# One decoder layer's dilated attention: the third group's blocks of 128 positions become pairs of 64, and the scheduler's transfer costs change

## The chip, the cores and the metric

One core of a Trainium2 chip runs the whole program. The metric is device time in microseconds of one execution, as a median of runs. Five engines work side by side and meet through semaphores: TensorE (PE, matrix products and transposes, with its weight loads as PEld), VectorE (DVE), ScalarE (ACT), GpSimd (POOL), and SyncE (SP), which only starts DMA transfers here.

## What is computed

A two-layer decoder trunk over 1024 positions of width 1024. Layer A is gated linear attention. Layer B, to which the change belongs, is dilated sliding-window attention of 8 query heads over 2 shared key and value heads, in three groups with windows 128, 512 and 2048 and dilations 1, 4 and 16. In each group the sequence is split into `dilation` interleaved sequences and each query sees the last `window // dilation` keys of its own; the groups' outputs are joined by a softmax over their log-sum-exps.

```python
def dilated_window_attention(q, k, v, window, dilation):
    ...
    scores = jnp.einsum('brnqgpe,brnkge->brngpqk', qb, kcat)
    ...
    band = (rel >= 0) & (rel <= w_sub)
    ...
    m = jnp.max(scores, axis=-1, keepdims=True)
    p = jnp.exp(scores - m)
    den = jnp.sum(p, axis=-1)
    o = jnp.einsum('brngpqk,brnkge->brnqgpe', p, vcat) / jnp.moveaxis(den, -1, 3)[..., None]
    lse = jnp.moveaxis(m[..., 0] + jnp.log(den), -1, 3)
    ...
```

```python
    wts = jax.nn.softmax(jnp.stack(lses, axis=0), axis=0)
    o = jnp.sum(wts[..., None] * jnp.stack(outs, axis=0), axis=0)
    o = o.reshape(bsz, s, SWA_OUT)
    return (o.astype(x.dtype) * jax.nn.silu(g)) @ w_out
```

With dilation 16 and 1024 positions, the third group has 16 sequences of 64 positions each, and its window covers a whole sequence: a query sees the keys of its own sequence up to itself, and no others.

## The kernel before

The program does not write its instruction order by hand. Every call (`S.tensor.matmul(...)`, `S.vector...`, `S.sync.dma_start(...)`) is recorded as an operation with the tiles it reads and writes, and `Sched.order` then plays the list through a model: each engine takes the ready operation that can start first, ties going to the earlier recorded one. `cost` gives each operation's duration in that model. A transfer's cost there is a size divided by a rate; the loop in `order` adds a landing time and a time for which SP is taken. The result is a fixed order on each engine; on the chip each engine then runs its list strictly in that order and waits wherever an input or a buffer is not there. Every emitted instruction carries the line of the one call that emits it, L441, so groups are told apart by tile names. `with S.group()` ties several calls into one operation, so that nothing comes between them.

A projection is a chain of float32r matmuls of 512 columns into a PSUM bank `acc`. Each product is split into three (`wh` times `x1h`, `wh` times `x1l`, `wl` times `x1h`), so a bank takes 24 of them. Attention products are float32 and are issued as two instructions each. Transposes go through TensorE in bfloat16 halves.

In layer B (`layer_b`) there are 8 units, one per query head. For unit u:

- `q_proj(u)` makes the queries Q of three groups; `rope` rotates them on VectorE and writes them, permuted to the group's order by `to_group`, on VectorE or GpSimd.
- `scores(u)` makes score blocks in PSUM (`lv`, two banks), adds the mask and takes the maximum on VectorE (the custom operation `P<-lv,rmask` for the third group), and exponentiates on ScalarE. Row maxima and sums go to DRAM and back (`sts`, `std`, `nat`), because groups order the positions differently, and come back as weights (`ew`, `cwd`, `cw`).
- `attend(u)` scales the blocks P by `cw`, turns them by transposes on TensorE (`ms<-identb,P`), copies the turned blocks out (`PT`), and multiplies with the values V into banks `po` (two). The third group's result is copied from `po` to `og` first; the first and second group then accumulate in the same two banks and are added to `og`.
- `g_proj(u)` and `close(u)` apply the gate.

The third group (`g == 2` in the code) puts two of the 16 sequences interleaved into one block of 128 positions: 8 blocks of 128 by 128, where the mask `rmask` hides every pair of positions of different sequences, half of the block. So a unit has 8 score products of 128 by 128, 16 transposes and 8 products with V of 128 by 128 for this group. Two score blocks' worth of banks and two rounds of turning are used (`step = 4`, `for hb in range(2)`).

At the end of the program `out_ln` makes the first half of the tokens with columns transposed, and `out_ln_rows` four blocks of 128 tokens (j = 4 to 7). A block has two banks of 24 matmuls each. Their results are added to the residual on VectorE (`rt<-res,acc`), measured (`BN_STATS`, `BN_AGGR`), normalised in two passes over two halves (`rt<-rt,lnmv,gam` and `rt<-rt,lnR,bet`) and sent out. For these blocks the output weight is split anew into `woh` and `wol`.

Of the kernel before, what the change touches and what calls it, by code (L numbers as in the profile page):

```python
# [139 lines left out]
class Sched:  # L140
# [108 lines left out]
    def order(self):  # L249
# [62 lines left out]
        while n_done < len(ops):  # L312
# [261 lines left out]
def trunk(tc, xT, wP, wA, wAv, wa, w2, b2, ng, wO, wK, wV, wB, wOB, lng, lnb,  # L574
# [534 lines left out]
    vd = [dram.tile([T, 256], F32, name=f"vd{i}") for i in range(2)]  # L1109
# [7 lines left out]
    def to_group(pg, g, half):  # L1117
        if g == 2:
            return pg.rearrange("p (b a n) -> p n a b", b=8, a=16)[:, half * 4:half * 4 + 4]
        n = 512 // DIL[g]  # L1120
        return pg.rearrange("p (r i) -> p i r", r=DIL[g])[:, half * n:half * n + n, :]

    def tok_view(ap, g):
        if g == 2:
            return ap.rearrange("p (n a b) -> p n a b", n=4, a=16)
        return ap.rearrange("p (i r) -> p i r", r=DIL[g])

    def layer_b(xs):
        bmask = hp.tile([128, 256], F32, name="bmask", bufs=1)
        S.sync.dma_start(bmask, bmask_d)  # L1130
        rmask = hp.tile([128, 128], F32, name="rmask", bufs=1)
# [29 lines left out]
        def proj_v(g):  # L1161
            stage = {}

            def evac(j, acc):
# [8 lines left out]
                if g == 2:  # L1173

                    S.sync.dma_start(vd[1].rearrange("(a n b) e -> n a b e", a=16, n=8)[j], dst)
                elif j % 4 == 3:
                    h = j // 4 * 512
                    S.sync.dma_start(vd[g - 1][h:h + 512, :].rearrange("(n p) e -> p n e", p=128),
                                      pg.rearrange("p (n e) -> p n e", n=4))
            project_tok(wV[g], xs, [(j, lambda x, j=j: blk(x, j)) for j in range(8)], evac)  # L1180

        def load_v(c, g):
            V[c][g] = page(p0, F32, f"V{c}{g}")
            src = vd[g - 1][:, c * 128:c * 128 + 128]
            if g == 1:
                for n in range(2):
                    S.sync.dma_start(
                        V[c][g].rearrange("p (r n e) -> p r n e", r=4, n=2)[:, :, n, :],
                        src[n * 512:n * 512 + 512, :].rearrange("(p r) e -> p r e", r=4))
# [29 lines left out]
        def reload_kv():  # L1219
            for g in range(3):  # L1220
# [10 lines left out]
              2: [(b * 128, b * 128, 128) for b in range(8)]}  # L1231
        U = [dict() for _ in range(8)]

# [20 lines left out]
        def scores(u):  # L1254
# [3 lines left out]
            for g in (2, 1, 0):  # L1258
                step = 4 if g == 2 else 2
                for j0 in range(0, 8, step):  # L1260
                    sc = ps.tile([128, 512], F32, name="lv", bufs=2)
                    p = small("P", "a", 13)
                    o = 0
                    for j in range(j0, j0 + step):
                        qc, kc, nk = BL[g][j]
                        col = column(g, j)
                        P[g, j] = p, o
# [16 lines left out]
            with S.landing(RUNS):  # L1284
# [3 lines left out]
                for s in range(2):  # L1288
                    S.sync.dma_start(dst[0, s].rearrange("(b a n) -> a b n", b=8, a=16), sts[:, s, 0:8])
                for s in range(2):  # L1290
                    S.sync.dma_start(nat[:, s, 1, :], dst[1, s].rearrange("(n a b) -> a n b", n=8, a=16))
            with S.landing(GATHER):
                for s in range(2):
                    S.sync.dma_start(nat[:, s, 0, :], dst[0, s].rearrange("(b p) -> p b", p=128))
# [17 lines left out]
            with S.landing(RUNS):  # L1312
                for g in range(2):
                    S.sync.dma_start(cwd[u][g].rearrange("(n a b) -> a n b", n=8, a=16), ew[:, g])
# [6 lines left out]
        def attend(u):  # L1321
# [153 lines left out]
def _arrays(inputs):  # L1475
# [54 lines left out]
    q, k = np.meshgrid(r(128), r(128), indexing="ij")  # L1530
    tq, tk = (128 * (i % 8) + 8 * (i // 8) for i in (q, k))
    a["rmask"] = np.where((tq % 16 == tk % 16) & (tk <= tq), f4(0), f4(NEG)).astype(f4)
# [28 lines left out]
```

## Time and profile before

| | |
|---|---|
| median of 3 runs | 1208.53 us (1208.48 to 1209.45) |
| the profiled execution | 1207.9 us |
| its span, first to last instruction | 1206.1 us |
| mean granted TensorE clock | 0.998 |
| PE busy | 1185.7 us, 98% of the span |
| PEld busy (beside PE) | 1017.2 us, 84% |
| DVE, ACT, POOL busy | 754.1, 529.9, 219.6 us |

The profiled execution's own time is 1.8 us over its span and 0.6 us under the median of the runs. Matmuls are pipelined: the printed duration of one (0.39 us for 512 columns) is its latency, and the time it takes from the engine is the distance from its start to the next start (0.23 us). A row of the timeline therefore tells its cost by the start of the row behind it.

### The profile page before, as it was taken

What the parts mean: (1) busy time and instruction counts of PE and PEld (TensorE: products, weight loads), DVE (VectorE), ACT (ScalarE), POOL (GpSimd) and SP (SyncE); (2) the same over time, 40 slices, a digit from 0 to 9 for tenths busy, and PEclk for the clock granted to TensorE, in tenths of its full rate; (3) what the DMA queues carried; (4) which work ended last, traced back from release to release, by engine and by line L of the source; (5) the groups of instructions that cost most, each with busy time, mean ns of one, the idle gap of its engine ahead of it and who ended that gap; (6) DMA issues with size and microseconds to landing.
All of it is one profiled execution on the core that took longest, in us unless ns stands there. A gap on an engine that the chain in (4) does not pass through costs nothing.

```text
span 1206.1 us, 20729 instructions
## 1 busy us (share of the span) xinstructions
PE 1185.7 (98%) x8340; PEld 1017.2 (84%) x8340; DVE 754.1 (63%) x1448; ACT 529.9 (44%) x1070; POOL 219.6 (18%) x145
## 2 busy tenths in 40 slices
PE   9999999999999999999999999999999999999996
PEld 7888978988988887789988888888888888888885
DVE  5482962943967698962255655564656566657468
ACT  5452534433563344422114554545362545456242
POOL 0011101211222122420031213040312130203200
PEclk9999999999999999999999999999999999999999
DMA  8102111111243462554411111111412020124545
GB/s 264 41 20 70 36 54 53 59 49 36 71 165 114 148 211 99 196 184 141 131 56 41 46 37 54 37 53 36 132 46 55 36 55 19 38 63 133 172 133 183
DMA packets 93648, 107.57 MB, mean 89 GB/s; under 512 B 43792, under 2 KB 63248, under 8 KB 93552
## 3 DMA queue, kind: packets, MB, share of 16 engines
q1 hardware_dynamic: 93552, 106.25, 28.3%
q8 instruction: 65, 1.06, 0.4%
q14 instruction: 31, 0.25, 0.1%
HBM read 85.06 MB, written 21.17 MB: 88 GB/s over the span
## 4 chain that ended last, share of the span: by engine, by line
PE 88%; DVE 8%; issue 2%; ACT 1%; DMA 1%; POOL 0%; SPq 0%; DVEq 0%; ACTq 0%; POOLq 0%
PE acc L441 62%; PE po L441 9%; PE lv L441 9%; PE ms L441 4%; PE pro L441 3%; DVE rt L441 2%; DVE X L441 2%; DVE wl L441 1%; DVE oT L441 1%; DVE x1l L441 1%; DMA xf<-in_xT 1%; ACT wh L441 0%; DMA cosT<-in_cos 0%; DVE t L441 0%; DVE sq L441 0%
## 5 line engine op out<-in xcount | busy, mean ns | idle before, releaser
L441 PE MATMUL acc<-x1h,wh 128*128 128x512 f32 x608 | 252.2, 415 | 2.0 <-DVE t L441 1.5
L441 PE MATMUL acc<-x1l,wh 128*128 128x512 f32 x608 | 237.5, 391 | 0.7 <-DVE x1l L441 0.6
L441 PE MATMUL acc<-x1h,wl 128*128 128x512 f32 x608 | 237.5, 391 | 0.0
L441 ACT ACTIVATE wh<-wf 128x1024 fp32r<-128x1024 f32 (+2 forms) x102 | 106.0, 1041 | 253.7 <-PE acc L441 201.6
L441 POOL TENSOR_TENSOR wl<-wf,wh 128x1024 fp32r<-128x1024 f32 x46 | 110.2, 2396 | 549.8 <-ACT wh L441 499.0
L441 PEld LDWEIGHTS acc<-x1h,wl 128*128 128x128 f32 x608 | 114.1, 188 | 24.4
L441 PEld LDWEIGHTS acc<-x1h,wh 128*128 128x128 f32 x608 | 114.5, 188 | 23.3 <-DVE t L441 2.0
L441 PEld LDWEIGHTS acc<-x1l,wh 128*128 128x128 f32 x608 | 114.5, 188 | 22.4 <-DVE x1l L441 1.7
L441 ACT ACTIVATE P<-P,sts 128x128 f32<-128x128 f32 (+1 forms) x192 | 84.9, 444 | 56.3 <-DVE sts L441 54.8
L441 DVE TENSOR_TENSOR wl<-wf,wh 128x1024 fp32r<-128x1024 f32 (+2 forms) x56 | 71.6, 1279 | 56.3 <-ACT wh L441 53.7
L441 DVE TENSOR_TENSOR t<-acc,cosT 128x512 f32<-128x512 f32 x60 | 41.3, 689 | 86.1 <-PE acc L441 79.7
L441 DVE TENSOR_TENSOR t<-acc,sinT 64x512 f32<-64x512 f32 x120 | 82.6, 688 | 2.0 <-ACT R L441 0.4
L441 PE MATMUL acc<-xh,wh 128*128 128x512 f32 x208 | 82.6, 397 | 0.0
L441 PE MATMUL acc<-xh,wl 128*128 128x512 f32 x208 | 81.1, 390 | 0.0
L441 PE MATMUL acc<-xl,wh 128*128 128x512 f32 x208 | 81.0, 389 | 0.0
L441 ACT ACTIVATE PT<-ms 128x512 uint16<-128x512 uint16 (+1 forms) x112 | 67.1, 679 | 30.1 <-PE ms L441 27.0
L441 PE MATMUL lv<-K,Q 128*128 128x256 f32 (+1 forms) x384 | 78.8, 324 | 0.0
L441 PE MATMUL acc<-wh,xh 128*128 128x256 f32 x256 | 75.6, 295 | 0.0
L441 PE MATMUL po<-PT,V 128*128 128x128 f32 (+1 forms) x464 | 73.3, 304 | 0.3 <-DVE PT L441 0.3
L441 DVE CUSTOM_DVE_ANT_0 P<-lv,bmask 128x256 f32<-128x256 f32 (+1 forms) x128 | 47.7, 382 | 40.3 <-PE lv L441 39.5
L441 PE MATMUL acc<-wl,xh 128*128 128x256 f32 x256 | 72.4, 283 | 0.3 <-issue 0.3
L441 PE MATMUL acc<-wh,xl 128*128 128x256 f32 x256 | 72.2, 282 | 0.0
(232 smaller groups left out, 2454.3 us busy)
## 6 DMA issues: line engine op xcount, KB each, us to landing
wf<-in_wB SPq DMA_DIRECT2D x32, 512.0 KB, 3.3
wf<-in_wO SPq DMA_DIRECT2D x16, 512.0 KB, 3.3
wf<-in_wOB SPq DMA_DIRECT2D x16, 512.0 KB, 3.8
wf<-in_wA SPq DMA_DIRECT2D x13, 512.0 KB, 3.2
wf<-in_wK SPq DMA_DIRECT2D x12, 512.0 KB, 3.4
wf<-in_wAv SPq DMA_DIRECT2D x8, 512.0 KB, 3.6
res<-in_xT SPq DMA_DIRECT2D x16, 256.0 KB, 2.7
wf<-in_wV SPq DMA_DIRECT2D x8, 512.0 KB, 3.8
```

Source lines behind the costliest of these rows:

```text
L441: getattr(handle[o.eng], meth)(*[conv(a) for a in args], **{k: conv(v) for k, v in kw.items()})
```

## The change

The third group's two sequences of a block are no longer interleaved. Its order of positions is now by sequence, so 16 pieces of 64 positions stand one behind another. Scores of a pair of sequences are two products of 64 by 64 that share the 128 rows of the contraction and write the lower and the upper 64 partitions of `lv`. All 16 stand in one group and one bank, in 8 blocks of 64 columns. Turning them takes 8 transposes, since a turned piece of 128 by 128 now holds four sequences. Products with V contract over 64 partitions: 16 products of 64 by 128 weights and 64 columns, alternating between the lower and the upper half of the partitions, each half writing its own `po` bank. Four copies of 256 columns take the place of two of 512. The mask is 64 columns wide.

The stores and loads that permute statistics and V follow the new order: V of the third group goes to two buffers of its own in DRAM, `nat` is loaded by 8 transfers rather than 4 per unit and `cwd` stored by 4 rather than 2. In the scheduler's model, transfers cost less time per byte, land sooner and take SP longer, and products that contract over 64 rows have a cost of their own.

```diff
@@ order
             if e == "SP":
                 dma_free = max(dma_free, st) + c
-                o.t1 = dma_free + 2.0
-                free[e] = st + 0.1
+                o.t1 = dma_free + 1.7
+                free[e] = st + 0.37
@@ cost
+        if args[1].shape[0] == 64:
+            return 0.12
         m = args[1].shape[1]
         return {32: 0.02, 64: 0.05}.get(m, 0.43)
     if e == "SP":
-        return 0.1 + int(_np.prod((outs + ins)[0].shape)) * 4 / 190e3
+        return 0.1 + int(_np.prod((outs + ins)[0].shape)) * 4 / 280e3
...
@@ to_group
         if g == 2:
-            return pg.rearrange("p (b a n) -> p n a b", b=8, a=16)[:, half * 4:half * 4 + 4]
+            return pg.rearrange("p (e a n) -> p n a e", e=16, a=8)[:, half * 4:half * 4 + 4]
...
@@ load_v
-                S.sync.dma_start(V[c][g].rearrange("p (b e) -> p b e", b=8),
-                                  src.rearrange("(p b) e -> p b e", b=8))
+                src = vd3[c].rearrange("(n a s k j) e -> k s a n (j e)", n=8, a=8, s=2, k=2)
+                for k in range(2):
+                    for s in range(2):
+                        S.sync.dma_start(V[c][g][k * 64:k * 64 + 64, s * 512:s * 512 + 512], src[k, s])
...
@@ scores
-                step = 4 if g == 2 else 2
+                step = 8 if g == 2 else 2
...
+                    if g == 2:
+                        with S.group():
+                            for j in range(8):
+                                for s in range(2):
+                                    x = s * 512 + j * 64
+                                    o = place(j)
+                                    S.tensor.matmul(sc[s * 64:s * 64 + 64, o:o + 64], Q[g][:, x:x + 64],
+                                                     Kc[g][:, x:x + 64], start=True, stop=True)
...
-                        S.tensor.matmul(sc[:, o:o + nk], Q[g][:, qc:qc + 128], Kc[g][:, kc:kc + nk],
-                                         start=True, stop=True)
+                        if g < 2:
+                            S.tensor.matmul(sc[:, o:o + nk], Q[g][:, qc:qc + 128], Kc[g][:, kc:kc + nk],
+                                             start=True, stop=True)
...
@@ attend
-            for hb in range(2):
-                t = turn([(4 * hb + s, 0) for s in range(4)], 2)
-                po = ps.tile([128, 512], F32, name="po", bufs=2)
-                for s in range(4):
-                    S.tensor.matmul(blk(po, s), blk(Vc[2], 4 * hb + s), t[:, s, :], start=True, stop=True)
-                S.vector.tensor_copy(og.rearrange("p (n a b) -> p a n b", n=8, a=16)[:, :, :, 4 * hb:4 * hb + 4],
-                                      po.rearrange("p (b a n) -> p a n b", b=4, a=16))
+            p, t = P[2, 0][0], small("PT", "d", 4)
+            turn_blocks(t, [p.halves(BF)[:, :, i * 128:i * 128 + 128] for i in range(4)])
+            po = [ps.tile([128, 512], F32, name="po", bufs=2) for _ in range(2)]
+            with S.group():
+                for s in range(2):
+                    for j in range(4):
+                        for k in range(2):
+                            h = slice(k * 64, k * 64 + 64)
+                            S.tensor.matmul(po[k][:, s * 256 + j * 64:s * 256 + j * 64 + 64],
+                                             blk(Vc[2], s * 4 + j)[h], t[h, j * 128 + s * 64:j * 128 + s * 64 + 64],
+                                             start=True, stop=True)
+            for k in range(2):
+                for s in range(2):
+                    x = s * 8 + k * 4
+                    S.vector.tensor_copy(
+                        og.rearrange("p (n a e) -> p n a e", n=8, a=8)[:, :, :, x:x + 4],
+                        po[k][:, s * 256:s * 256 + 256].rearrange("p (j a n) -> p n a j", j=4, a=8))
...
```

**Where instructions stand.** First TensorE, in `attend` of unit 0, with the scores of unit 1 among it (`ms<-identb,P` are transposes, `po<-PT,V` products with V, `lv<-K,Q` scores, `acc` projections). Before:

```order
L441 MATMUL acc<-x1h_4468,wl 128x512
L441 MATMUL po<-PT,V_6118 128x128 x4
...
L441 MATMUL po<-PT,V_6118 128x128 x4
...
L441 MATMUL po<-PT,V_5795 128x128 x3
L441 MATMUL lv<-K_5040,Q 128x128
...
L441 MATMUL po<-PT,V_5795 128x128 x9
```

Now, from the same projection on:

```order
L441 MATMUL acc<-x1h_4468,wl 128x512
...
L441 MATMUL po<-PT,V_6070 128x64 x16
...
L441 MATMUL lv<-K_5045,Q 64x64 x16
L441 MATMUL po<-PT,V_5732 128x128 x12
...
L441 MATMUL lv<-K_4967,Q 128x128 x2
```

The lines left out are transposes: 6 and 12 and 6 before; 6 ahead of and 12 behind the `128x64` products now. All of the third group's products with V now stand in one piece, and the next unit's third-group scores in another, ahead of the second group's first use of the `po` banks.

Then VectorE, at the same place in unit 0. Before:

```order
L441 TENSOR_TENSOR t_6672<-acc,cosT 128x512
L441 TENSOR_TENSOR t_6687<-acc,sinT 64x512 x2
L441 COPY og<-po 128x16x8x4 x2
L441 COPY PT<-ms 128x384 x2
L441 ISA P,sts<-lv,rmask 128x128
```

Now:

```order
L441 TENSOR_TENSOR t_6684<-acc,cosT 128x512
L441 TENSOR_TENSOR t_6697<-acc,sinT 64x512 x2
L441 COPY PT<-ms 128x384
L441 TENSOR_TENSOR Q<-t_6684,t_6697 128x4x8x16
L441 COPY og<-po 128x64x4 x4
L441 ISA P,sts<-lv,rmask 128x64
```

The permuted write of the third group's Q has come from GpSimd to VectorE, ahead of the copies that set the `po` banks free.

Last VectorE at the end of the program, the last rows of its list. Before:

```order
L441 SCALAR_TENSOR_TENSOR rt<-res,acc 128x512
L441 BN_STATS lnst<-rt 128x6
L441 BN_AGGR lnmv<-lnst 128x2
L441 SCALAR_TENSOR_TENSOR rt<-rt,lnmv,gam 128x512 x2
L441 SCALAR_TENSOR_TENSOR rt<-rt,lnR,bet 128x512 x2
L441 BN_AGGR lnmv<-lnst 128x2
L441 SCALAR_TENSOR_TENSOR rt<-rt,lnmv,gam 128x512 x2
L441 SCALAR_TENSOR_TENSOR rt<-rt,lnR,bet 128x512 x2
```

Now:

```order
L441 SCALAR_TENSOR_TENSOR rt<-res,po 128x512
L441 BN_STATS lnst<-rt 128x6
L441 SCALAR_TENSOR_TENSOR rt<-rt,lnmv,gam 128x512 x2
L441 SCALAR_TENSOR_TENSOR rt<-rt,lnR,bet 128x512 x2
L441 SCALAR_TENSOR_TENSOR rt<-res,acc 128x512
L441 BN_STATS lnst<-rt 128x6
L441 BN_AGGR lnmv<-lnst 128x2
L441 SCALAR_TENSOR_TENSOR rt<-rt,lnmv,gam 128x512 x2
L441 SCALAR_TENSOR_TENSOR rt<-rt,lnR,bet 128x512 x2
```

Behind the last matmuls' result (`rt<-res,acc`) two blocks were normalised; now it is one. The splits `wol<-wf,woh`, of which five stood behind `sum<-lnA,sum` on VectorE, have moved: three stand there now.

## Rows read from the trace of the kernel before

**Rows 1.** Page: busy time, share and count by engine; chain's shares by engine.
```profile
PE 1185.7 (98%) x8340; PEld 1017.2 (84%) x8340; DVE 754.1 (63%) x1448; ACT 529.9 (44%) x1070; POOL 219.6 (18%) x145
...
PE 88%; DVE 8%; issue 2%; ACT 1%; DMA 1%; POOL 0%; SPq 0%; DVEq 0%; ACTq 0%; POOLq 0%
```

**Rows 2.** Chain that ended last, in order of time: start us, us, what.
```profile
710.96 32.68 PE acc L441 x144
...
1075.43 18.39 PE acc L441 x81
...
1097.80 1.82 DVE P L441 x4
```

**Rows 3.** Timeline of PE, third group's scores: start us, us, instructions merged.
```profile
634.86 0.60 PE L441 MATMUL lv<-K,Q 128*128 128x128 f32 x4
...
636.00 0.60 PE L441 MATMUL lv<-K,Q 128*128 128x128 f32 x4
```

**Rows 4.** Timeline of PE, third group's turning and products with V.
```profile
679.67 1.07 PE L441 MATMUL ms<-identb,P 128*128 128x128 bf16 x16
680.54 0.48 PE L441 MATMUL acc<-x1h,wh 128*128 128x512 f32 x1
...
682.04 1.16 PE L441 MATMUL po<-PT,V 128*128 128x128 f32 x8
683.03 0.50 PE L441 MATMUL ms<-identb,P 128*128 128x128 bf16 x6
683.37 1.11 PE L441 MATMUL po<-PT,V 128*128 128x128 f32 x8
684.32 0.86 PE L441 MATMUL ms<-identb,P 128*128 128x128 bf16 x12
```

**Rows 5.** Timeline of PE, layer A: eight 64 by 64 products on two column halves.
```profile
308.44 0.28 PE L441 MATMUL acc<-wh,xl 128*128 128x256 f32 x1
308.64 0.69 PE L441 MATMUL lv<-X 128*64 128x64 f32 x16
...
309.48 0.28 PE L441 MATMUL acc<-wl,xh 128*128 128x256 f32 x1
```

**Rows 6.** Groups by form: engine, rows*columns, size, xcount | busy us, mean ns | idle.
```profile
L441 PE MATMUL lv<-X 128*64 128x64 f32 x64 | 2.7, 227 | 1.9 <-DVE X L441 1.9
...
L441 PEld LDWEIGHTS lv<-X 128*32 128x32 f32 x1408 | 15.5, 110 | 6.4 <-issue 2.7 <-ACT X L441 1.7
...
L441 PEld LDWEIGHTS po<-PT,V 128*128 128x128 f32 x464 | 64.6, 191 | 8.3 <-ACT PT L441 4.2 <-DVE PT L441 0.5
```

**Rows 7.** Groups by form: copies out of PSUM, and GpSimd's permuted write of Q.
```profile
L441 DVE COPY v<-acc 128x256 f32<-128x256 f32 x16 | 6.6, 413 | 0.2 <-PE acc L441 0.2
...
L441 DVE COPY og<-po 128x512 f32<-128x512 f32 x16 | 11.0, 690 | 14.5 <-PE po L441 14.5
...
L441 POOL TENSOR_TENSOR Q<-t,t 128x512 f32<-128x512 f32 x17 | 21.9, 1288 | 34.4 <-DVE t L441 34.4
```

**Rows 8.** Timeline of VectorE and TensorE at the program's end, last matmul last.
```profile
1195.88 0.68 DVE L441 SCALAR_TENSOR_TENSOR rt<-res,acc 128x512 f32<-128x512 f32 x1
...
1197.43 1.41 DVE L441 SCALAR_TENSOR_TENSOR rt<-rt,lnmv,gam 128x512 f32<-128x512 f32 x2
1198.76 1.41 DVE L441 SCALAR_TENSOR_TENSOR rt<-rt,lnR,bet 128x512 f32<-128x512 f32 x2
1200.09 0.20 DVE L441 BATCH_NORM_AGGREGATE lnmv<-lnst 128x2 f32<-128x12 f32 x1
...
1201.66 1.41 DVE L441 SCALAR_TENSOR_TENSOR rt<-rt,lnR,bet 128x512 f32<-128x512 f32 x2
...
1195.37 0.39 PE L441 MATMUL acc<-woh,ogl 128*128 128x512 f32 x1
```

**Rows 9.** A late stretch: its length, busy us of PE, PEld, DVE, ACT, POOL, clock.
```profile
1180.00:1196.00 16.00, 15.76 (x70) 12.72 (x68) 15.80 (x28) 4.64 (x9) 0.00 (x0) 1.00 0.56 196
```

**Rows 10.** Timeline of SP: one issue of a transfer.
```profile
1175.39 0.34 SPq L441 DMA_DIRECT2D res<-x1t  x1
```

More of the change, by code (lines that the diff above doesn't have):

```diff
@@ L1107, in trunk @@
     kvd = [dram.tile([128, T], F32, name=f"kvd{i}") for i in range(4)]
-    vd = [dram.tile([T, 256], F32, name=f"vd{i}") for i in range(2)]
+    vd = dram.tile([T, 256], F32, name="vd")
+    vd3 = [dram.tile([T, 128], F32, name=f"vd3{c}") for c in range(2)]
     ogB = [dram.tile([128, T], F32, name=f"ogB{k}") for k in range(NK)]
@@ L1124, in tok_view @@
         if g == 2:
-            return ap.rearrange("p (n a b) -> p n a b", n=4, a=16)
+            return ap.rearrange("p (n a e) -> p n a e", n=4, a=8)
         return ap.rearrange("p (i r) -> p i r", r=DIL[g])
@@ L1130, in layer_b @@
         S.sync.dma_start(bmask, bmask_d)
-        rmask = hp.tile([128, 128], F32, name="rmask", bufs=1)
+        rmask = hp.tile([128, 64], F32, name="rmask", bufs=1)
         S.sync.dma_start(rmask, rmask_d)
@@ L1172, in evac @@
                     S.vector.tensor_copy(dst, acc)
-                if g == 2:
-                    S.sync.dma_start(vd[1].rearrange("(a n b) e -> n a b e", a=16, n=8)[j], dst)
-                elif j % 4 == 3:
+                if j % 4 == 3:
                     h = j // 4 * 512
-                    S.sync.dma_start(vd[g - 1][h:h + 512, :].rearrange("(n p) e -> p n e", p=128),
-                                      pg.rearrange("p (n e) -> p n e", n=4))
+                    rows = pg.rearrange("p (n e) -> p n e", n=4)
+                    if g == 1:
+                        S.sync.dma_start(vd[h:h + 512, :].rearrange("(n p) e -> p n e", p=128), rows)
+                    else:
+                        for c in range(2):
+                            S.sync.dma_start(vd3[c][h:h + 512, :].rearrange("(n p) e -> p n e", p=128),
+                                              rows[:, :, c * 128:c * 128 + 128])
             project_tok(wV[g], xs, [(j, lambda x, j=j: blk(x, j)) for j in range(8)], evac)
@@ L1183, in load_v @@
             V[c][g] = page(p0, F32, f"V{c}{g}")
-            src = vd[g - 1][:, c * 128:c * 128 + 128]
             if g == 1:
@@ L1230, in layer_b, with place @@
               1: [(r * 256 + n * 128, r * 256, 128 + 128 * n) for r in range(4) for n in range(2)],
-              2: [(b * 128, b * 128, 128) for b in range(8)]}
+              2: [(b * 64, b * 64, 64) for b in range(8)]}
         U = [dict() for _ in range(8)]
+        def place(b):
+            return b % 4 * 128 + b // 4 * 64
         def column(g, j):
@@ L1288, in scores @@
                 for s in range(2):
-                    S.sync.dma_start(dst[0, s].rearrange("(b a n) -> a b n", b=8, a=16), sts[:, s, 0:8])
+                    S.sync.dma_start(dst[0, s].rearrange("(e a n) -> a e n", e=16, a=8), sts[:, s, 0:8])
                 for s in range(2):
-                    S.sync.dma_start(nat[:, s, 1, :], dst[1, s].rearrange("(n a b) -> a n b", n=8, a=16))
-            with S.landing(GATHER):
+                    for i in range(2):
+                        S.sync.dma_start(nat[i * 64:i * 64 + 64, s, 1, :],
+                                          dst[1, s].rearrange("(n a i b) -> i a n b", n=8, a=8, i=2)[i])
+            with S.landing(GATHER / 2):
                 for s in range(2):
-                    S.sync.dma_start(nat[:, s, 0, :], dst[0, s].rearrange("(b p) -> p b", p=128))
+                    for i in range(2):
+                        S.sync.dma_start(nat[i * 64:i * 64 + 64, s, 0, :],
+                                          dst[0, s].rearrange("(i b p) -> i p b", i=2, b=8)[i])
             mn = hp.tile([128, 8], F32, name="mnB", bufs=1)
@@ L1313, in scores @@
                 for g in range(2):
-                    S.sync.dma_start(cwd[u][g].rearrange("(n a b) -> a n b", n=8, a=16), ew[:, g])
+                    for i in range(2):
+                        S.sync.dma_start(cwd[u][g].rearrange("(n a i b) -> i a n b", n=8, a=8, i=2)[i],
+                                          ew[i * 64:i * 64 + 64, g])
             with S.landing(GATHER):
@@ L1529, in _arrays @@
     a["bmask"] = np.where((rel >= 0) & (rel <= 128), f4(0), f4(NEG)).astype(f4)
-    q, k = np.meshgrid(r(128), r(128), indexing="ij")
-    tq, tk = (128 * (i % 8) + 8 * (i // 8) for i in (q, k))
-    a["rmask"] = np.where((tq % 16 == tk % 16) & (tk <= tq), f4(0), f4(NEG)).astype(f4)
+    q, k = np.meshgrid(r(128) % 64, r(64), indexing="ij")
+    tq, tk = (128 * (i % 8) + 16 * (i // 8) for i in (q, k))
+    a["rmask"] = np.where(tk <= tq, f4(0), f4(NEG)).astype(f4)
     return a
```

4 lines of the change are left out of this document (3 added, 1 removed).

## The prediction

> **What bounds the kernel now.** I read the page's busy times first: TensorE is busy for 1185.7 of 1206.1 us, and the chain that ended last lies on it for 88% [rows 1]. A busy TensorE need not be one that is used without gaps, so next I read its timeline for the distances from start to start. In the chain, 144 projection matmuls follow each other in 32.68 us [rows 2], 0.227 us each, and that is what they cost wherever I looked in layer B. There is hardly a place there where the engine waits: in the units' stretches the next instruction's inputs are there before the one ahead is through. So in layer B a microsecond taken from TensorE is a microsecond of the program, if nothing that now hides behind it comes out. The exception is the end: the last matmul starts at 1195.37, VectorE takes up its result at 1195.88 and works until 1201.66 + 1.41 = 1203.07 [rows 8]. In the 16 us up to that point VectorE is busy for 15.80 [rows 9]. So VectorE sets the end there, and the order of its list counts.
>
> **Scores of the third group.** Before, two of the eight products with three projection matmuls behind them take 636.00 - 634.86 = 1.14 us [rows 3]; less 3 x 0.227 that is 0.46 for two, 1.84 for eight. The new products have a relative in layer A that is the same in form: 64 by 64 with 128 rows of contraction, alternating between two column halves. Eight of them (16 instructions) stand between matmuls of 256 columns. From the start of the last such matmul ahead of them to that of the second behind them is 309.48 - 308.44 = 1.04 us [rows 5]; without the group these two starts would be two steps of 0.12 us apart, 256 columns at half of the 0.227 for 512 and a little, so the group costs 0.80. Of it, (0.69 - 0.227) / 15 = 0.031 us is what one more instruction adds [rows 5, 6], and 0.80 - 16 x 0.031 = 0.31 is what it costs to go to halves and back. Two halves at once are seen here: an instruction of 128 columns takes 0.46 / 4 = 0.115 above, so one of 64 would take some 0.06 if alone. Sixteen products are 32 instructions: 0.80 + 16 x 0.031 = 1.30. Gain 0.54 a unit; with twice the whole group's price (1.60) it would be 0.24.
>
> **Transposes.** Sixteen take 680.54 - 679.67 = 0.87 us [rows 4], 0.054 each. Eight are left out: gain 0.43 a unit. Half the copies of turned blocks go too, on ScalarE, beside TensorE: nothing.
>
> **Products with V.** Before: 0.99 and 0.95 us for four each [rows 4], 1.94 for the eight, 0.121 per instruction. After: 32 instructions with half the columns, half the contraction and a full-width weight load (64 rows by 128 columns) each. No row of the trace shows products on two row halves. The bounds: as good as two column halves, 32 x 0.031 + 0.31 = 1.30; no better than now per instruction, 32 x 0.121 + 0.31 = 4.18. What lies between is told by the weight loads. They last 110 ns for 32 columns and 191 ns for 128 [rows 6], 0.84 ns for each column, so some 0.108 us for 128 columns if only the part that grows with the columns occupies the array. That is nearly the 0.121 that a full-size instruction takes now, so halving the columns that stream through cannot bring the distance down as long as one half is loaded at a time. If the two row halves load and compute beside each other, as the two column halves do, a pair takes what one instruction takes now: 16 x 0.121 + 0.31 = 2.25. I take this value, a loss of 0.31 a unit, because halves of the array are seen to run together in the one direction that is shown, while the load stays full width.
>
> The Trainium skill, "TensorE: Matmul & The Clock Gate", section "LDWEIGHTS (loading the stationary operand)", speaks against this part of the change: a load takes about its columns divided by 1.2 in ns, whether 32 or 128 rows are filled. The trace agrees on the columns (0.84 ns each), and says nothing on the rows. By this rule alone, with loads one behind another, the 32 loads would take an estimated 3.4 us, and the sum below would come out slower than before.
>
> A unit then gains 0.54 + 0.43 - 0.31 = 0.66 us, and eight units 5.3 us.
>
> **What must stay hidden.** (a) The two `po` banks. Both are now held until four copies of 256 columns have passed, and the second group's products come next. TensorE has 12 transposes (0.65) and the next unit's third-group scores (1.30) ahead of them, 1.95 us. The copies start about 0.2 after the products, as now, and take 4 x 0.413 [rows 7]: the first bank is free after 1.0 us, the second after 1.85, wanted after 2.2. Covered, by 0.3. (b) The write of Q, 1.29 us on GpSimd so far [rows 7], now stands on VectorE ahead of those copies; from the start of the turning to the end of the products it is 684.32 - 679.67 = 4.65 us in the trace [rows 4], and it is done within them if it takes VectorE no longer than GpSimd: covered too. (c) Six more transfers of statistics and weights a unit, 0.34 us each to issue [rows 10]: 2.1 us more, in a path that lies on the chain in the last unit alone, where four scalings of P by `cw` on VectorE follow a run of 81 projection matmuls [rows 2]. There the changed list has 99 of them as cover: 18 x 0.227 = 4.1 us more. Covered. (d) The refitted costs of transfers act through order alone. Up to layer B the lists are almost the same, with shifts of three matmuls where TensorE already waits for the layer norm; I set this at nothing, with 1 us either way.
>
> **The end.** Behind the last result VectorE normalises two blocks before and one now. What goes from behind it is one pair of passes, 1200.09 - 1197.43 = 2.66 us [rows 8]. That holds if VectorE is not late by then: it has two splits of weights fewer in the last 40 us, and the block ahead has its two passes (2.7 us) and one result to take up (two instructions of 0.7) in the 5.4 us of the last bank's 24 matmuls. I take the 2.66 whole; the bounds are 0 and 2.66.
>
> Sum: 5.3 + 2.7 = 8.0 us off 1207.9, so 1199.9 for an execution like the profiled one; the runs' median stands 0.6 above that one, so **1200.5 us**.
>
> **Rivals.**
> *The halves cost no more than column halves.* Products with V take 1.30: a unit gains 0.54 + 0.43 + 0.64 = 1.61, eight 12.9, with the end 15.6: 1192.9. For it: the same array, the same number of passes, and the loads of column halves do overlap. Against it: there the loads are half as wide.
> *The row halves take turns.* 32 x 0.121 + 0.31 = 4.18 for V, a loss of 2.24 a unit: 2.24 - 0.97 = 1.27 more a unit, 10.2 in all, less the end's 2.7: 1216.0, slower. The change would then not do what its name says. The point from which it decides: 32p + 0.31 must exceed 1.94 + 0.97 + 0.33 (an eighth of the end), which is p = 0.092 us per instruction. For it: the loads' width and the price above. Against it: the column halves do run together.
> *The copies uncover `po`.* If a copy of 256 columns with its strided write takes as long as one of 512 (0.69) [rows 7], the second bank is free after 0.2 + 4 x 0.69 = 2.96 us, 0.77 later than wanted; eight units lose 6.2, and the time is 1206.7, no change. A late write of Q on VectorE would act in the same way. Against it: 512 columns in the same kind of pattern take the same 0.69 as plain copies do.
> *The end is not shortened* (VectorE late): 1203.2, still faster; this lies in the forecast's range.
>
> **How the numbers follow.** The forecast with its scatter (1197 to 1204) has 0.55, the cheap halves 0.17, the turns 0.16, the uncovered banks 0.12. About 0.2% (2.4 us) is what a measurement of this kernel can tell from no change. Faster by more takes the forecast, the cheap halves and the better part of the third: 0.77. Within: most of the rest of the uncovered banks, 0.08. Slower: 0.15. The range leaves out the turns and a little of the others: 1191.5 to 1208.
>
> **What would show it.** In the changed profile: the third group's 32 score instructions 0.03 us apart; the 32 products with V 0.06 apart on average (0.03 or 0.12 in the rivals); eight transposes fewer a unit; no idle time of TensorE ahead of `po<-PT,V 128x128` with VectorE's `og` copies as its end; last VectorE instruction ending 4.5 us after the last result is taken up, not 7.2. The prediction is wrong in kind if TensorE begins to wait in the units for statistics or for Q.

## The result, and the profile after

| | before | after |
|---|---|---|
| median | 1208.99 us (1208.48 to 1209.57, 4 runs) | 1201.92 us (1200.40 to 1202.50, 4 runs) |
| ratio | | 0.9939, 95% interval 0.9922 to 0.9957 |
| the profiled execution | 1207.9 | 1202.5 |
| its span | 1206.1 | 1200.6 |
| mean granted TensorE clock | 0.998 | 0.995 |

The kernel became 7.1 us faster by the medians. The two profiled executions differ by 5.5 us in span; they are one run each, and the one of after is among its slower ones. The start of the program alone varies by up to 1.8 us between executions of one list: the 500th matmul of 512 columns starts at 195.98 us here and at 194.18 in `e8_quarters_priced`, whose lists are the same up to there.

The page of after, busy time by engine, which answers [rows 1]:

```profile
PE 1179.5 (98%) x8532; PEld 1008.6 (84%) x8532; DVE 777.4 (65%) x1480; ACT 515.1 (43%) x1061; POOL 188.7 (16%) x122
```

**A unit.** The timeline of TensorE in unit 0's `attend`, with the scores of the next unit behind it (columns as in [rows 3, 4]: start us, us, merged instructions):

```profile
684.53 0.49 PE L441 MATMUL ms<-identb,P 128*128 128x128 bf16 x6
684.95 2.00 PE L441 MATMUL po<-PT,V 64*128 64x64 f32 x32
686.89 0.84 PE L441 MATMUL ms<-identb,P 128*128 128x128 bf16 x12
687.66 1.15 PE L441 MATMUL lv<-K,Q 128*64 128x64 f32 x32
688.74 2.94 PE L441 MATMUL po<-PT,V 128*128 128x128 f32 x24
```

From start to start the 32 products with V take 686.89 - 684.95 = 1.94 us, 0.061 each. The trace starts them in pairs: two instructions 7 ns apart, then 105 ns to the next two, 0.111 us a pair. The 32 score instructions take 1.08 us, 0.034 each. No row shows TensorE waiting.

How long a whole unit takes is read from the chain that ended last, where the long run of projections comes back once a unit (start us, us, what). After:

```profile
709.08 36.08 PE acc L441 x159
...
771.92 36.07 PE acc L441 x159
...
834.76 36.08 PE acc L441 x159
```

That is 62.84 us twice. Before, the run of 144 that starts at 710.96 [rows 2] comes back at 774.78, after 63.82 us. A unit gives 0.98 us. Summing all start-to-start distances of one such unit by kind shows where:

| in one unit, us | before | after | gain |
|---|---|---|---|
| products with V, third group | 2.06 (16 instructions) | 1.93 (32) | 0.12 |
| scores, third group | 1.50 (16) | 1.08 (32) | 0.42 |
| transposes | 3.92 (70) | 3.65 (62) | 0.27 |
| projections (the same 192) | 45.55 | 45.26 | 0.29 |
| everything else of groups 1 and 2 | 10.80 | 10.91 | -0.11 |

(The V row of before is the difference of 46 and 30 instructions of one form, the score row that of 26 and 10.) The projections are the same matmuls; they lose fewer switches, since the third group stands in one piece instead of being spread among them.

**Where time was lost.** The 3428 matmuls of 512 columns are the same in both kernels, so the start of the n-th can be compared. At the 1250th (470 us) after is 0.35 us ahead. At the 1310th (486 us) it is 4.52 behind, by the first scores 3.04 behind. Eight units bring it to 4.96 ahead (1099 us), and the last matmul starts 3.24 ahead. In between lie two places where TensorE waits. The first is layer B's layer norm. TensorE's waits from 440 to 520 us (what waits, for whom: us in total, times, longest), before:

```profile
PE acc L441 <- DVE t L441: 1.5, 2, 1.1
PE ms L441 <- POOL sum L441: 1.1, 1, 1.1
```

and after:

```profile
PE ms L441 <- DVE sum L441: 2.0, 1, 2.0
PE acc L441 <- DVE t L441: 1.7, 2, 1.0
PE ms L441 <- ACT sum L441: 1.4, 1, 1.4
```

VectorE's list there has changed: two splits of weights (`wl<-wf,wh`) come ahead of `rt<-rt,mean`, and the last sum runs on VectorE while GpSimd splits weights. Windows of the same place (length, busy us of PE, PEld, DVE, ACT, POOL, granted clock, DMA), before:

```profile
477.00:483.00 6.00, 6.00 (x29) 4.93 (x28) 5.88 (x9) 2.45 (x4) 0.90 (x1) 1.00 0.27 91
```

and after:

```profile
470.00:477.00 7.00, 3.60 (x15) 2.48 (x13) 5.73 (x7) 2.21 (x3) 2.35 (x1) 0.93 0.23 75
477.00:483.00 6.00, 5.37 (x13) 3.86 (x14) 5.65 (x10) 1.94 (x3) 0.00 (x0) 0.51 0.28 87
```

TensorE was idle for half of 470 to 477, and behind that, from 477 to 483, its clock was granted at 0.51, the 1.2 GHz level; ten matmuls stand 0.427 us apart there instead of 0.227. The second place is the last unit, where the four copies out of `po` stand behind seven scalings of P. After, TensorE's and VectorE's timelines:

```profile
1095.71 0.49 PE L441 MATMUL ms<-identb,P 128*128 128x128 bf16 x6 [0.38 <-ACT PT L441]
1096.93 0.49 PE L441 MATMUL po<-PT,V 128*128 128x128 f32 x2 [0.72 <-DVE og L441]
1097.59 0.71 PE L441 MATMUL po<-PT,V 128*128 128x128 f32 x4 [0.17 <-DVE og L441]
```

```profile
1091.47 4.75 DVE L441 TENSOR_SCALAR P<-P,cw 128x128 f32<-128x128 f32 x7
1096.13 1.41 DVE L441 COPY og<-po 128x256 f32<-128x256 f32 x4
```

**The end**, which answers [rows 8]:

```profile
1192.13 0.39 PE L441 MATMUL acc<-woh,ogl 128*128 128x512 f32 x1
```

```profile
1192.56 0.69 DVE L441 SCALAR_TENSOR_TENSOR rt<-res,acc 128x512 f32<-128x512 f32 x1 [0.77 <-PE acc L441]
1193.28 0.69 DVE L441 BATCH_NORM_STATS2 lnst<-rt 128x6 f32<-128x512 f32 x1
1194.01 0.21 DVE L441 BATCH_NORM_AGGREGATE lnmv<-lnst 128x2 f32<-128x12 f32 x1
1194.25 1.42 DVE L441 SCALAR_TENSOR_TENSOR rt<-rt,lnmv,gam 128x512 f32<-128x512 f32 x2
1195.58 1.41 DVE L441 SCALAR_TENSOR_TENSOR rt<-rt,lnR,bet 128x512 f32<-128x512 f32 x2
```

VectorE ends 1196.99 - 1192.56 = 4.43 us after it takes up the last result, 7.19 before [rows 8]. It now waits 0.77 us for that result, so it is no longer late.

The ledger of the two profiled executions, in us gained: 0.35 up to the layer norm, -3.4 at the layer norm and until the first scores, +8.0 in the units, -1.7 from there to the last matmul, +2.8 in VectorE's end, -0.6 behind it. Sum 5.5.

### The profile page after: what moved, and what is told of

The parts are those of the page before. It is cut to its first block, busy times and chain, and to the rows that moved or that the text cites. A ratio compares the mean times of both kernels' runs of the same rounds, so it can differ in the third digit from the quotient of the medians.

```text
span 1200.6 us, 21156 instructions
## 1 busy us (share of the span) xinstructions
PE 1179.5 (98%) x8532; PEld 1008.6 (84%) x8532; DVE 777.4 (65%) x1480; ACT 515.1 (43%) x1061; POOL 188.7 (16%) x122
## 4 chain that ended last, share of the span: by engine, by line
PE 53%; DVE 2%; DMA 1%; issue 1%; ACT 0%; DVEq 0%
PE acc L441 38%; PE po L441 7%; PE lv L441 6%; PE ms L441 3%; DMA wf<-in_wOB 1%; DVE P L441 0%; DVE rt L441 0%; DVE wol L441 0%; ACT woh L441 0%; DVE t L441 0%; DVE wl L441 0%; DVE PT L441 0%; DVE og L441 0%; DVE lnA L441 0%; DVE lnst L441 0%
## 5 line engine op out<-in xcount | busy, mean ns | idle before, releaser
L441 POOL TENSOR_TENSOR wl<-wf,wh 128x1024 fp32r<-128x1024 f32 x45 | 107.7, 2395 | 608.0 <-ACT wh L441 573.6
L441 DVE TENSOR_TENSOR wl<-wf,wh 128x1024 fp32r<-128x1024 f32 (+2 forms) x57 | 74.2, 1302 | 67.0 <-ACT wh L441 66.5
L441 ACT ACTIVATE P<-P,sts 128x128 f32<-128x128 f32 (+2 forms) x192 | 81.0, 429 | 40.4 <-DVE sts L441 40.1
L441 ACT ACTIVATE PT<-ms 128x384 uint16<-128x384 uint16 (+1 forms) x106 | 60.7, 659 | 33.8 <-PE ms L441 30.0
L441 PE MATMUL po<-PT,V 64*128 64x64 f32 (+2 forms) x592 | 70.4, 295 | 0.9 <-DVE og L441 0.9
L441 PEld LDWEIGHTS po<-PT,V 128*128 128x128 f32 (+1 forms) x592 | 62.6, 189 | 7.0 <-DVE og L441 1.3
```

The source lines that it names most:

```text
L441: getattr(handle[o.eng], meth)(*[conv(a) for a in args], **{k: conv(v) for k, v in kw.items()})
```

## The experiments

The first question is which part of the change did what: the new blocks, or the planner's new prices for transfers, which move the order of everything. Three kernels and the changed one ran on one chip beside the kernel before (median there 1208.81 us).

**The changed kernel as the mark (`e0_after`).** 

> The changed kernel once more, beside the next three on one chip, as the mark that they are measured against. Expected 1201.9 us, 7 us under the kernel before.

Measured: 1201.20 us, ratio 0.9942 (0.9930 to 0.9955). As expected.

**The new blocks with the old transfer costs (`e1_old_costs`).**

```diff
-                o.t1 = dma_free + 1.7
-                free[e] = st + 0.37
+                o.t1 = dma_free + 2.0
+                free[e] = st + 0.1
...
-        return 0.1 + int(_np.prod((outs + ins)[0].shape)) * 4 / 280e3
+        return 0.1 + int(_np.prod((outs + ins)[0].shape)) * 4 / 190e3
```

> The blocks changed, the planner's transfer costs left as before. Theory (read from the two traces): the new blocks give 8.0 us in the units, 1.00 a unit; the refitted costs take 3.0 back ahead of layer B (a longer wait for the layer norm and a lower clock behind it) and give 2.8 at the end. With the old costs the wait is as before; the end lies between, since VectorE's list has one pass pair more (1.33 us) behind the last result than the changed kernel's: 1201.9 - 3.0 + 1.3 = 1200.2. Rival (the prediction's account: costs act at the end only, 2.7 us there): 1203.2 for this list, 1204.6 if the whole end comes back. In the trace: TensorE's start of layer B's first third-group scores 3 us earlier than in the changed kernel by the theory, at the same time by the rival.

Measured: 1204.42 us, ratio 0.9965 (0.9953 to 0.9977). The number is nearer to the rival's, but not for its reason. Up to 494 us its lists are, engine by engine, those of the kernel before. The layer norm's waits are nearly those of before again (1.1 us for the sum on GpSimd, 1.9 for VectorE's `t`, where before has 1.1 and 1.5), and the clock is 1.00 from 477 to 483 us:

```profile
477.00:483.00 6.00, 5.71 (x25) 4.75 (x26) 5.45 (x9) 2.40 (x4) 0.00 (x0) 1.00 0.24 74
```

The unit is 62.86 us, as in the changed kernel; its chain:

```profile
708.00 36.08 PE acc L441 x159
...
770.86 36.08 PE acc L441 x159
```

So these two steps of the theory hold. What it did not see is the last unit. TensorE's waits from 1085 to 1125 us:

```profile
PE ms L441 <- ACT PT L441: 1.9, 2, 1.1
PE acc L441 <- DVE ogl L441: 1.7, 2, 1.5
PE acc L441 <- ACT ogh L441: 1.2, 1, 1.2
PE po L441 <- ACT PT L441: 0.2, 1, 0.2
```

5.0 us, where the changed kernel waits 1.3 there. The chain of that stretch runs through the loads of gated heads back from DRAM:

```profile
1088.80 2.70 DMA ogf<-ogB
...
1093.67 5.18 DMA ogf<-ogB
```

With the old prices the planner puts work that needs these loads ahead of the turned P. The refitted prices earn their gain here. That is a matter of the order that comes out and not of the old prices as such: with the blocks of before, the same prices leave 0.6 us of waits in the last unit.

**The old blocks with the refitted costs (`e2_before_new_costs`).**

```diff
-                o.t1 = dma_free + 2.0
-                free[e] = st + 0.1
+                o.t1 = dma_free + 1.7
+                free[e] = st + 0.37
...
-        return 0.1 + int(_np.prod((outs + ins)[0].shape)) * 4 / 190e3
+        return 0.1 + int(_np.prod((outs + ins)[0].shape)) * 4 / 280e3
```

> The blocks as before, the planner's transfer costs refitted. Theory: 3.0 us lost ahead of layer B, 2.8 won at the end, units as before: 1209.0 + 0.2 = 1209.2, no change. Rival (the prediction's account, costs act at the end only): 1209.0 - 2.7 = 1206.3. Second rival, that the refit is where the whole gain comes from: 1202.

Measured: 1206.14 us, ratio 0.9978 (0.9970 to 0.9987). Faster, where the theory said no change, and at the rival's number. Up to 499 us its lists are, engine by engine, those of the changed kernel. The trace has the theory's two steps: TensorE is 3.65 us late at the first scores, with the clock at the lower level from 477 to 483, and stays so through the units (no gain in them); VectorE's end is the changed kernel's.

```profile
477.00:483.00 6.00, 5.37 (x12) 3.90 (x13) 5.69 (x9) 1.84 (x3) 0.00 (x0) 0.50 0.26 87
```

But it also has no wait of TensorE at all in the last unit, where before shows 0.6 us for PT and more in small pieces; that gives 1.65 back. The profiled execution accounts for 1.0 of the 2.7; the rest was not located in it.

So the gain is in two nearly additive parts: blocks alone 4.4 us, costs alone 2.7, sum 7.1, both together 7.6 on this chip. Each part is itself a sum of both signs.

**The layer norm's wait taken back (`e6_costs_switched`).**

```diff
-                dma_free = max(dma_free, st) + c
-                o.t1 = dma_free + 1.7
-                free[e] = st + 0.37
+                dma_free = max(dma_free, st) + 0.1 + (c - 0.1) * (280 / 190 if st < 560 else 1)
+                o.t1 = dma_free + (2.0 if st < 560 else 1.7)
+                free[e] = st + (0.1 if st < 560 else 0.37)
```

> The changed kernel with the old transfer costs in the planner up to 560 us of its own time (VectorE's list is then that of the kernel before up to the first units) and the refitted ones behind. Theory: the wait ahead of layer B is that of before, the units and the end those of the changed kernel: 1201.9 - 3.0 = 1198.9. Rival: the wait ahead of layer B is work that is due anyway and comes back later: 1201.9.

Measured: 1200.95 us, ratio 0.9927 (0.9915 to 0.9940), beside 1201.20 (0.9942, 0.9930 to 0.9955). The waits are nearly those of before and the clock stays at 1.00:

```profile
477.00:483.00 6.00, 5.95 (x26) 4.95 (x27) 5.45 (x8) 2.41 (x4) 0.00 (x0) 1.00 0.20 55
```

In the trace TensorE is 1.9 us earlier at the first scores than in `e0_after`, of the 3 expected, since this execution loses 0.9 elsewhere ahead of them. Most of that is one wait of 0.69 us at 338 us that comes and goes between executions of one list: `e7_quarters_switched`, whose lists are the same up to there, does not have it. The spans differ by 2.0, the means of the runs by 1.6, the medians by 0.25; the intervals overlap. That the longer wait and the lower clock behind it cost some 3 us is shown in the trace: from the 1000th matmul of 512 columns to the first scores `e0_after` loses 3.9 us against the kernel before, `e6_costs_switched` 0.5. That taking them away makes the kernel faster is not shown by the runs.

The second question is how the products on the two row halves go. Theory C, as in the prediction: the halves run beside each other, and a load of 128 columns occupies its half for 0.11 us. L: loads one behind another at half that price. T: the halves take turns at half the old price, because only half the columns stream.

**The halves in runs (`e3_rows_in_runs`).**

```diff
-                for s in range(2):
-                    for j in range(4):
-                        for k in range(2):
+                for k in range(2):
+                    for s in range(2):
+                        for j in range(4):
```

> The changed kernel, with the 16 products with V in another order: first the eight of the lower row half, then the eight of the upper, instead of taking turns. Everything else, the other engines' lists too, is the same. Three theories on the 0.111 us that a pair (one instruction of each half) takes in the changed trace. C, the halves load and compute beside each other, and a load of 128 columns occupies its half for 0.108 us: without a neighbour on the other half each of 32 instructions takes 0.11, 1.7 us more a unit, 14 in all: 1215.9. L, loads go one behind another at half that price (0.053 us each) and only the streams run beside each other: unchanged if a load hides behind the stream of the same half, 1201.9, up to 1215.9 if it can't. T, the halves take turns, and an instruction of 64 columns takes 0.055 because it streams half the columns: unchanged, 1201.9.

Measured: 1218.27 us, ratio 1.0089 (1.0061 to 1.0117), 16 to 17 us slower than the changed kernel (1201.92 and 1201.20). The same place of TensorE's timeline as above:

```profile
684.98 3.48 PE L441 MATMUL po<-PT,V 64*128 64x64 f32 x32
688.40 1.46 PE L441 MATMUL ms<-identb,P 128*128 128x128 bf16 x12
689.79 1.94 PE L441 MATMUL lv<-K,Q 128*64 128x64 f32 x32
```

The 32 instructions take 3.42 us, 0.107 each, instead of 1.94 (3.32 in the five units in which the clock stays at 1.00); within a run they stand 0.112 us apart. That a run writes one `po` bank does not explain it: the 32 score instructions of the changed kernel all write one bank too, and stand 0.034 us apart. T falls: without a neighbour on the other half one instruction of 64 columns takes as long as a pair. C holds; L would need that a load can't hide behind the same half's stream. A unit takes 64.2 us instead of 62.8, 9.7 us in seven units; the last unit adds nothing, TensorE is 15.8 us behind the changed kernel both before and after its products with V. In three of the eight units 1.5 to 3 us come on top, in the two rows behind: 12 transposes take 1.39 us instead of 0.77, the scores 1.87 instead of 1.08. The windows show why, the granted clock fell:

```profile
684.90:688.30 3.40, 3.40 (x35) 3.30 (x32) 2.33 (x4) 1.12 (x3) 0.84 (x1) 0.98 0.44 141
688.30:691.70 3.40, 3.40 (x46) 3.03 (x45) 0.76 (x2) 1.95 (x4) 0.00 (x0) 0.52 0.06 20
```

The Trainium skill, "TensorE: Matmul & The Clock Gate", section "Part 3: Packing small matmuls — row/col tiling", says that a weight load overlaps with matmuls in flight only when it goes to another group of rows. The two kernels agree as far as the halves go: 0.112 us each on one half, 0.111 for two on both. They do not bear out the "only": `e4_128_columns` below streams twice the columns through each half in the same 0.111 us a pair. Were a load and the stream of its own half one behind the other, the pair would have grown, so they overlap too.

**Twice the columns through the same weights (`e4_128_columns`).** In 14 of the 16 products the columns that are streamed include 64 of the next piece; the next product overwrites what they give.

```diff
-                            S.tensor.matmul(po[k][:, s * 256 + j * 64:s * 256 + j * 64 + 64],
-                                             blk(Vc[2], s * 4 + j)[h], t[h, j * 128 + s * 64:j * 128 + s * 64 + 64],
+                            x, y = s * 256 + j * 64, j * 128 + s * 64
+                            n = 128 if (s, j) < (1, 3) else 64
+                            S.tensor.matmul(po[k][:, x:x + n], blk(Vc[2], s * 4 + j)[h], t[h, y:y + n],
                                              start=True, stop=True)
```

> The changed kernel, with 128 instead of 64 columns streamed through each set of weights in 14 of the 16 products with V (the 64 behind them are overwritten by the next product). The loads stay, the streams double. C: a pair stays at 0.111 us, since the load sets it: 1201.9. L: the two streams of 0.107 us run beside each other, a pair stays at 0.11: 1201.9. T: 14 of 16 pairs go from 0.111 to 0.22, 1.55 us a unit and 12.4 in all: 1214.3.

Measured: 1201.36 us, ratio 0.9939 (0.9923 to 0.9956).

```profile
684.46 2.00 PE L441 MATMUL po<-PT,V 64*128 64x128 f32 x32
686.39 0.84 PE L441 MATMUL ms<-identb,P 128*128 128x128 bf16 x12
```

1.93 us, as with 64 columns. The streamed columns set nothing here: T falls again, and what is left as the limit is the load.

**Quarters of the array (`e5_quarters`).**

```diff
-                            S.tensor.matmul(po[k][:, s * 256 + j * 64:s * 256 + j * 64 + 64],
-                                             blk(Vc[2], s * 4 + j)[h], t[h, j * 128 + s * 64:j * 128 + s * 64 + 64],
-                                             start=True, stop=True)
+                            for c in range(0, 128, 64):
+                                S.tensor.matmul(po[k][c:c + 64, s * 256 + j * 64:s * 256 + j * 64 + 64],
+                                                 blk(Vc[2], s * 4 + j)[h, c:c + 64],
+                                                 t[h, j * 128 + s * 64:j * 128 + s * 64 + 64],
+                                                 start=True, stop=True)
```

(In the planner such a product costs 0.06 instead of 0.12, so the order stays.) 

> The changed kernel, with each of the 16 products with V split into two of 64 weight columns, so that four quarters of the array take the products in turn: 64 instructions instead of 32, half as wide loads, the same columns streamed in each. C: loads of half the width take half as long and four quarters run at once: 16 x 0.054 = 0.87 us instead of 1.78, 0.9 us a unit, 7.3 in all: 1194.6. L: 64 loads of 0.027 us one behind another, 1.71 us: no change, 1201.9. T: column halves side by side, row halves in turns, 32 x 0.055: no change, 1201.9; if all four take turns, 64 x 0.055 = 3.5, 1.75 a unit: 1215.9.

Measured: 1196.39 us, ratio 0.9898 (0.9883 to 0.9913), 5 us faster than the changed kernel.

```profile
685.11 1.16 PE L441 MATMUL po<-PT,V 64*64 64x64 f32 x64
686.21 0.84 PE L441 MATMUL ms<-identb,P 128*128 128x128 bf16 x12
```

64 instructions take 1.10 us, four of them 0.058 us once under way. Twice as many loads in 0.57 of the time: L falls, and C is what is left of the three. (Whether at 64 by 64 the load or the stream of 64 columns sets the 0.058 is open.) A unit takes 62.03 us, 0.8 less; 6.4 in all, of which 5.5 arrive in the medians (1201.92 and 1196.39), since the last unit now waits 2.0 us instead of 1.3.

**Can more be had from the quarters?** Two variants beside the same kernel again, on one chip.

**The mark (`e5_again`).** 

> The kernel with products on quarters of the array once more, as the mark for the next two on one chip: 1196.4 us, as measured, 0.990 of the kernel before.

Measured: 1195.88 us, ratio 0.9891 (0.9877 to 0.9906). As before.

**Quarters with the switched costs (`e7_quarters_switched`)**: the edit of `e6_costs_switched` on `e5_quarters`. 

> Quarters of the array, and the planner's old transfer costs up to 560 us of its own time, the refitted ones behind. Theory: the two gains are on different stretches and add up. In the traces TensorE reached the units 1.7 us earlier with the switched costs than with the refitted ones, and the medians of the pair differed by 0.3 (1201.2 and 1200.95): 1194.7 to 1196.1. Rival: what comes earlier ahead of the units is waited for in the last unit, where the quarters' kernel already waits 2.1 us for P and PT: 1196.4.

Measured: 1196.23 us, ratio 0.9895 (0.9881 to 0.9910): the rival's number, no gain. At the layer norm TensorE loses 1.6 us where `e5_again` loses 2.9: the waits are those of before, but this time the clock fell behind them too, if for a shorter time (0.76 from 477 to 483 us). And in the last unit, where both kernels wait for some 2 us, the clock fell in `e7_quarters_switched` and not in `e5_again`. Its windows there:

```profile
1086.00:1090.50 4.50, 2.63 (x75) 1.93 (x66) 4.50 (x8) 4.50 (x13) 3.23 (x3) 1.00 0.88 273
1090.50:1095.00 4.50, 4.45 (x29) 4.12 (x29) 3.51 (x9) 2.40 (x6) 1.28 (x1) 0.62 0.59 208
```

**Quarters with their own price (`e8_quarters_priced`).**

```diff
         if args[1].shape[0] == 64:
-            return 0.06
+            return 0.035
```

> Quarters of the array with the price that the trace shows in the planner: 0.035 us for each of the 32 products instead of 0.06 (the group of 64 instructions took 0.94 + 0.15 us). Theory: the price acts through order alone, and a list closer to what runs places the last unit's work better; of the 2.1 us of waits there up to 2 go: 1194.4. Rival: orders differ by chance, as the transfer costs showed (3 us lost in one place, 4 won in another): anywhere within 3 us of 1196.4.

Measured: 1193.23 us (1190.77 to 1195.76), ratio 0.9877 (0.9860 to 0.9893). The waits of the last unit, 1080 to 1120 us, are nearly gone:

```profile
PE ms L441 <- ACT PT L441: 0.3, 1, 0.3
```

This is the lowest median of the study, 15.6 us under the kernel before and some 8 under the changed one. Against `e5_again` the intervals overlap, and one list doesn't tell a better price from a lucky order, so that the price is the cause is not shown. Of the 3.9 us by which the last matmul of its profiled execution comes ahead of that of `e5_again`, 1.4 are there ahead of the units already, where the lists of the two are the same.

## Why the prediction came out right, step by step

**The total** was 1200.5; measured were 1201.9 and, on another chip, 1201.2. It is right within its scatter, but several of its terms were off and cancelled, and that they did is luck: in the profiled executions the units and the end gave 10.8 us where 8.0 were worked out, and the layer norm, the last unit and what stands behind VectorE's end, all set at nothing, took back some 5.4.

**Scores** (gain 0.54): right as a difference, 0.42 in their own distances and part of the 0.29 that the projections lose in switches. The 0.034 us per instruction is near the 0.031 of layer A [rows 5, 6]; the group took 1.08 us, not 1.30.

**Transposes** (gain 0.43): 0.27 in their own distances. The eight are gone, at 0.056 us each, but the last transpose ahead of each of the two new groups pays for a switch: 0.149 us to the group's first instruction instead of 0.056. The term didn't have that.

**Products with V** (loss 0.31): the mechanism was right, the size was off by 0.43 us a unit in their own distances, and this is the term that moved the units' sum most. They became 0.12 cheaper. A pair takes 0.111 us, and that is what one whole-array instruction took before: within a group those stood 0.112 us apart, and the 0.121 of the working holds the longer first step of each group (0.165 to 0.213 us) as well. So a switch was counted twice, in the 0.121 and in the 0.31. The way in and out costs 0.15 in the group's own distances; taken as layer A's 0.31 was, with the transposes on either side, it is 0.25. And the 16 of before cost 2.06, with their own switches, not 1.94. The argument from the width of the load stands: it is what `e3_rows_in_runs`, `e4_128_columns` and `e5_quarters` show. The section of the Trainium skill that spoke against the change ("TensorE: Matmul & The Clock Gate", "LDWEIGHTS (loading the stationary operand)") had the price of one load right: its rule gives 128 / 1.2 = 107 ns, and instructions in a run on one half stand 0.112 us apart; the 3.4 us estimated from it is near what the runs of one half took, 3.32 to 3.42. But loads on two halves don't stand behind one another: 1.94.

**A unit** (gain 0.66): 0.98. Eight gave 8.0 us instead of 5.3.

**What must stay hidden.** (a) The `po` banks were free in time in seven units: VectorE's four copies ran from 686.99 to 688.41, the second group's products start at 688.74, a margin of 0.33 where 0.3 was worked out. That the margins agree is luck: the copies were through 1.52 us behind the products and not 1.85, and TensorE wanted the banks after 1.85 us and not 2.2. In the last unit it failed, 0.9 us, by something that the step didn't look at: there scalings of P stand ahead of the copies. (b) Q's write on VectorE: covered. (c) The statistics' six more transfers: covered in the units; TensorE has no wait from 640 to 1085 us. (d) "The refitted costs of transfers act through order alone. Up to layer B the lists are almost the same, with shifts of three matmuls where TensorE already waits for the layer norm; I set this at nothing, with 1 us either way." This step failed. The list of VectorE at the layer norm was different in a few rows that mattered, and put TensorE 3.0 us behind at the first scores, some 2 of them by the lower clock behind the wait (ten matmuls 0.2 us longer each). `e1_old_costs` and `e2_before_new_costs` show that the costs do it and the blocks don't. In the last unit the same costs are worth 3.7 us of waits the other way with the new blocks, and 1.65 us of time with the old ones.

**The end** (2.66): 2.76 in VectorE's list, 2.8 from the last matmul on. The prediction left open which edit it came from: the refitted costs, by `e2_before_new_costs`, where the end is the changed kernel's, with the blocks of before.

**The rivals.** Row halves in turns: excluded by 0.061 us per instruction, under the 0.092 from which it would decide. Row halves as cheap as column halves: not so, 0.061 against 0.034; the weights are twice as wide. Uncovered `po`: in one unit of eight, by the scalings and not by slow copies. End not shortened: it was shortened, by 2.8.

## What to carry to other kernels

Where small float32 products like these are put on parts of TensorE, count the loads by the columns of their weights and by the part they go to. Here loads on different parts ran beside each other (0.111 us a pair), loads on one part queued (0.112 each), and narrower weights on more parts beat wide ones on few (1.10 us against 1.94). Alternate the parts instruction by instruction. And where a planner's prices are changed together with the work, judge each alone: here the price moved 3 us at the layer norm and several the other way in the last unit and at the end, places that the edit of the work never touched.

## What was not expected of the hardware

TensorE's clock fell without any idle time. In `e3_rows_in_runs` it issued products back to back from 684.98 to 688.40, but on one half of the array at a time, and from 688.30 to 691.70 the granted clock was 0.52, the 1.2 GHz level. It fell so in three of the eight units of the profiled run (at 688, 818 and 948 us); why in these and not in the other five is open. With the halves alternating, and with quarters, it stayed at 1.00 in every unit, but for the stretch behind the waits in the last unit of `e7_quarters_switched`. Elsewhere in these traces it fell behind waits only, and not by their length alone: the same list with the same waits at the layer norm kept 1.00 in `e6_costs_switched` and had 0.76 from 477 to 483 us in `e7_quarters_switched`.

Doubling the columns streamed through a half of the array, from 64 to 128 in float32, cost nothing here: 1.93 us against 1.94 for the group.
